# Pooling stage: plain float32 for the group map and for the first half-token up-products, and GpSimd's large operations there on VectorE

## The chip, the cores and the metric

The kernel runs on one core of a Trainium2 chip. The metric is the device time of one execution in microseconds (us); lower is better. The engines have short names in the profile: PE is TensorE's matmul, PEld its weight load, DVE is VectorE, ACT is ScalarE, POOL is GpSimd, SP is the engine that issues the DMAs here.

## What is computed

One step of a two-layer decoder for 512 prompt tokens and 8 sample tokens (520 columns). Layer 0 is a gated linear recurrence (HGRN2), layer 1 a causal pooling mixer; each is followed by a feed-forward with a squared ReLU. All of it is float32. The parts that the change touches:

```python
def _pool(x, hist, start, norm_g, w_grp, scale):
    u = _rmsnorm(x, norm_g)
    ...
    for gi, w in enumerate(POOL_WINDOWS):              # (2, 4, 8, 16), 256 channels each
        ...                                            # trailing-window means of u
        parts.append((hi - lo) / cnt)
    z = (pooled - u)                                   # in 4 groups of 256 channels
    y = jnp.einsum('blgc,gcd->blgd', z, w_grp) * scale
    return y, ext[:, -P:]

def _mlp(x, norm_g, w_up, w_down):
    h = _rmsnorm(x, norm_g)
    a = jnp.square(jax.nn.relu(jnp.einsum('bld,df->blf', h, w_up)))
    return jnp.einsum('blf,fd->bld', a, w_down)

x = x + y;  x = x + _mlp(...)                          # each layer
return _rmsnorm(x, final_norm), ...
```

The group map is linear, so the kernel maps the unpooled channels first, and takes the window means of the mapped rows.

## The kernel before

**Layout.** Channels lie on the 128 partitions, in 8 tiles (`NT`); the 520 columns (`T`) are tokens, in two halves of 260 (`HT`). `x` stays on the chip for the whole run. All weights come as chunks of 128x1024 float32 (512 KB) from one tensor, `wall`, in the order that `_order()` writes out.

**Products.** A product in float32 is made of three fp32r matmuls (`mm3`): both operands are split into a high part (rounded to fp32r) and a low part (the rest), and high·high, high·low and low·high are added up in PSUM. `split()` takes a loaded chunk `w` (pool `raw`, three buffers): ScalarE casts the high part `wh` in two halves, and an engine subtracts for the low part `wl`, VectorE where the second entry of `_order()` is False, GpSimd where it is True. Activations are split in the same way: `split_norm` (gain times `x`, into `u`), `up_part` (into `a`), `unpooled` (into `zh`, `zl`). Split weights and activations share 24 slots of SBUF.

**Order.** `_Mix` is a counter in program time: every few matmuls `tick()` runs what is due of the side work (generators that yield how many ticks to wait), and `top_up()` loads and splits the next chunks. TensorE's order is the order in the program. VectorE's, ScalarE's, GpSimd's and SP's order is written by hand only in the first layer's mixer; from the first feed-forward on a scheduler sets it.

**The stretch in question** starts in the last down-products of the first feed-forward. They are made for one half of the tokens at a time (`pr`, four PSUM buffers), seven or eight for the first half, then eight for the second (three of whose chunks, `AGAIN`, are loaded and split once more). After each, `after_mlp0` adds the squares for the pooling norm (`squares`, sums on GpSimd) and splits the unpooled channels (`unpooled`); after every second one `mapped` does the group map, 12 matmuls for 2x2 tiles. When a half is complete, `rstd` takes the mean by a matmul with `mean_w`, the root on ScalarE and the reciprocal on VectorE (1 / root, `r_p`), and `windows` runs four times: it multiplies by `r_p`, subtracts from `x`, adds shifted copies (1 to 4 adds, `s`), adds the scaled sum to `x`, splits `x` times gain into `u1`, and sums squares for the next norm (`r_m`).

**The second feed-forward** begins with its first group for one half of the tokens at a time: eight up-products of the first half (`up_part`: after the product, VectorE multiplies relu by `r_m` into `t`, ScalarE squares it and casts the high part of `a`, VectorE subtracts the low part), then three down-products (`SOON`) of the first half, then the eight up-products of the second half, with the same up chunks loaded and split a second time. From there on whole products of 520 columns follow.

Lines that the steps of the prediction touch: matmuls L270 and L321 (`mean_w`), `wh` L199, `wl` L194, sums L313, reciprocal L326, `zl` L860, multiplication L889, subtraction L890, window adds L896, scaled sum L899, `u` L297 and L298, `t` L773 and L774, `a` L775 and L776, down-product's add L783.

## Time and profile before

| | us |
|---|---|
| median of 3 runs | 1128.67 |
| lowest and highest | 1127.41, 1131.13 |
| the profiled execution | 1129.82 |
| its span, first to last instruction | 1128.0 |

Over the span PE is busy 1085.1 us (96%), DVE 664.0 (59%), ACT 445.7 (40%), POOL 177.1 (16%). The mean granted clock of TensorE is 0.983 of full speed. Times in the trace count from the first instruction. A busy time is the union of the engine's instructions; a row of a timeline begins with its start and its duration, and ends, in brackets, with how long the engine sat idle before it and what ended that. A DVE instruction's duration reaches some 0.08 us into the next one, so work is best added up from start to start.

### The profile page before, as it was taken

The page shows a single profiled execution, that of the slowest core. Times are in us where ns is not written, and L with a number is a line of the kernel's source. Part 1 is how long each engine was busy: PE and PEld are TensorE (multiplying, and loading weights), DVE is VectorE, ACT ScalarE, POOL GpSimd, SP SyncE. Part 2 cuts the span into 40 slices and gives each one's busy share as a digit, 9 for nine tenths or more (in the row PEclk, how much of TensorE's full clock was granted, in tenths as well). Part 3 has the DMA queues.
Part 4 walks back from the last instruction along what each step waited for, and adds up shares of the span by engine and source line. Part 5 has one row for each costly group of instructions (what it writes and reads, how often), then busy time and mean ns, then how long its engine had stood idle before and what let it go on. Part 6 is the DMA issues. An engine that isn't in the chain of part 4 may idle for free.

```text
span 1128.0 us, 21309 instructions
## 1 busy us (share of the span) xinstructions
PE 1085.1 (96%) x8794; PEld 1071.7 (95%) x8794; DVE 664.0 (59%) x1254; ACT 445.7 (40%) x954; POOL 177.1 (16%) x211
## 2 busy tenths in 40 slices
PE   9899999899999999999999999788999999999996
PEld 8899999899999999999999999687999999999996
DVE  7888888888566433643452466897524524533454
ACT  6544554444344322421431462645514413412442
POOL 1011110011002131322120025584100000000000
PEclk9999999999999999999999999887999999999998
DMA  8233323222244553664461361133512412331212
GB/s 267 77 103 110 98 94 100 80 96 97 80 136 130 184 172 102 182 186 132 156 191 54 103 197 39 57 97 117 183 57 76 144 64 76 110 115 57 94 57 76
DMA packets 67169, 128.13 MB, mean 114 GB/s; under 512 B 8256, under 2 KB 36608, under 8 KB 67072
## 3 DMA queue, kind: packets, MB, share of 16 engines
q1 hardware_dynamic: 67072, 126.77, 35.3%
q8 instruction: 69, 1.13, 0.4%
q14 instruction: 28, 0.23, 0.1%
HBM read 119.71 MB, written 7.50 MB: 113 GB/s over the span
## 4 chain that ended last, share of the span: by engine, by line
PE 73%; DVE 17%; ACT 4%; issue 2%; DMA 1%; POOL 0%; DVEq 0%; POOLq 0%; ACTq 0%
PE acc L270 61%; PE pr L270 10%; DVE A L477 3%; DVE wl L194 2%; DVE s L896 1%; DVE Y L423 1%; DVE z L381 1%; PE pr L472 1%; ACT wh L199 1%; DVE X L423 1%; DMA st<-s 1%; DVE u L298 1%; ACT W L451 1%; DVE W L423 1%; DVE bc L593 1%
## 5 line engine op out<-in xcount | busy, mean ns | idle before, releaser
L270 PE MATMUL acc<-u,wh 128*128 128x260 f32 x2208 | 362.2, 286 | 0.8 <-ACT u L297 0.4
L270 PEld LDWEIGHTS acc<-u,wh 128*128 128x128 f32 x2208 | 304.0, 188 | 2.4 <-DVE u L298 0.8
L270 PE MATMUL acc<-u,wl 128*128 128x260 f32 x1104 | 221.9, 282 | 0.0
L194 DVE TENSOR_TENSOR wl<-w,wh 128x512 fp32r<-128x512 f32 x252 | 179.0, 746 | 40.3 <-ACT wh L199 39.5
L199 ACT CAST wh<-w 128x512 fp32r<-128x512 f32 x276 | 156.2, 617 | 110.3 <-DMA w<-wall 67.4
L270 PEld LDWEIGHTS acc<-u,wl 128*128 128x128 f32 x1104 | 169.8, 188 | 0.0
L270 PE MATMUL acc<-a,wh 128*128 128x260 f32 x1024 | 164.0, 282 | 0.0
L270 PEld LDWEIGHTS acc<-a,wh 128*128 128x128 f32 x1024 | 140.1, 188 | 0.0
L773 DVE SCALAR_TENSOR_TENSOR t<-acc,r 128x520 f32<-128x520 f32 x56 | 39.1, 698 | 120.6 <-PE acc L270 120.5
L774 ACT ACTIVATE t<-t 128x520 f32<-128x520 f32 (+1 forms) x72 | 42.3, 588 | 168.8 <-DVE t L773 168.8
L199 ACT CAST wx<-w 128x512 fp32r<-128x512 f32 x82 | 46.8, 619 | 153.9 <-PE acc L270 150.2
L783 DVE TENSOR_TENSOR x<-x,acc 128x520 f32<-128x520 f32 x48 | 33.3, 694 | 125.2 <-PE acc L270 125.2
L270 PE MATMUL acc<-u,wx 128*128 128x260 f32 x864 | 106.3, 282 | 0.0
L270 PEld LDWEIGHTS acc<-u,wx 128*128 128x128 f32 x864 | 104.6, 188 | 0.0
L270 PE MATMUL acc<-a,wl 128*128 128x260 f32 x512 | 102.9, 282 | 0.0
L270 PE MATMUL acc<-a,wx 128*128 128x260 f32 x768 | 94.6, 282 | 0.0
L270 PEld LDWEIGHTS acc<-a,wx 128*128 128x128 f32 x768 | 93.1, 188 | 0.0
L776 DVE TENSOR_TENSOR a<-t,a 128x520 fp32r<-128x520 f32 (+1 forms) x72 | 48.6, 677 | 58.4 <-ACT a L775 58.4
L270 PEld LDWEIGHTS acc<-a,wl 128*128 128x128 f32 x512 | 78.7, 188 | 0.0
L270 PE MATMUL pr<-a,wh 128*128 128x260 f32 x384 | 71.8, 288 | 0.0
L270 PEld LDWEIGHTS pr<-a,wh 128*128 128x128 f32 x384 | 61.0, 194 | 0.1
L616 POOL TENSOR_TENSOR st<-st,bc 128x512 f32<-128x512 f32 x16 | 21.6, 1348 | 237.8 <-DMA bc<-rows 237.8
(211 smaller groups left out, 1495.1 us busy)
## 6 DMA issues: line engine op xcount, KB each, us to landing
w<-wall SPq DMA_DIRECT2D x181, 512.0 KB, 3.4
st<-s SPq DMA_DIRECT2D x32, 256.0 KB, 3.3
bc<-rows SPq DMA_DIRECT2D x32, 256.0 KB, 6.6
bc<-rows SPq DMA_DIRECT2D x16, 258.0 KB, 3.2
ss_o<-st SPq DMA_DIRECT2D x16, 256.0 KB, 4.2
x<-xT SPq DMA_DIRECT2D x8, 260.0 KB, 5.3
y_o<-pe SPq DMA_DIRECT2D x8, 260.0 KB, 2.6
W<-msk SPq DMA_DIRECT2D x3, 192.0 KB, 6.1
```

The costliest lines, as they stand in the source:

```text
L194: (nc.gpsimd if engine else nc.vector).tensor_tensor(wl[:, k], w[:, k], wh[:, k], op=ALU.subtract)
L199: nc.scalar.copy(wh[:, k], w[:, k])
L270: nc.tensor.matmul(o, lhs[a], r[b], start=first and n == 0, stop=last and n == 2)
L298: nc.vector.scalar_tensor_tensor(u[1][:, s], x[:, i, s], gc, u[0][:, s], op0=ALU.mult, op1=ALU.subtract)
L381: nc.vector.tensor_tensor(wide(z, h), a, wide(r1, h), op=ALU.mult)
L423: nc.vector.tensor_tensor(out, a, R.unsqueeze(len(out.shape) - 1).broadcast_to(out.shape), op=ALU.mult)
L477: nc.vector.copy_predicated(Av[:, jj * kk:(jj + 1) * kk, d:4, :].rearrange("p k s b -> p k (s b)"), mv[:, :, s:s + n, :].rearrange("p k s ...
L616: nc.gpsimd.tensor_tensor(st, st, tf, op=ALU.mult)
L773: nc.vector.scalar_tensor_tensor(wide(t, h), acc, 0.0, wide(r, h), op0=ALU.max, op1=ALU.mult)
L774: nc.scalar.activation(t[:, s], t[:, s], AF.Square)
L776: nc.vector.tensor_tensor(a[m][1][:, s], t[:, s], a[m][0][:, s], op=ALU.subtract)
L783: nc.vector.tensor_tensor(xs, xs, acc, op=ALU.add)
```

## The change

The group map and the eight up-products of the second feed-forward's first group, first token half, become single matmuls in plain float32: the pooling weights are loaded into two tiles of their own and not split, the unpooled channels are one tile `zp` of float32, the first-half `u` is a float32 tile `u32`, and the up chunks of this pass stay whole in their raw buffer until the product is done (`whole_w`). The split of the first half's `u`, which the later groups still need, is made afterwards, as side work (`first_half`). What GpSimd did in this stretch, the low parts of some weights, the sums of squares, the first half's multiplication and all subtractions of `windows`, goes to VectorE; the second entry of `_order()` now says whether a chunk is split.

```diff
-    out = [(i, False) for i in range(down + 2)]
+    out = [(i, True) for i in range(down + 2)]
     out += [(pool + c, None) for c in range(2)]
-    out += [(i, False) for i in range(down + 2, pool)]
+    out += [(i, True) for i in range(down + 2, pool)]
     out += [(i, True) for i in range(down, down + AGAIN)]
-    out += [(mlp1 + m, m > 2) for m in range(G)]
+    out += [(mlp1 + m, False) for m in range(G)]
     out += [(mlp1 + G + m, True) for m in range(SOON)]
-    out += [(mlp1 + m, m % 2 == 0) for m in range(G)]
-    out += [(i, False) for i in range(mlp1 + G + SOON, mlp1 + n)]
+    out += [(mlp1 + m, True) for m in range(G)]
+    out += [(i, True) for i in range(mlp1 + G + SOON, mlp1 + n)]
...
     def load():
         if order:
-            i, engine = order.pop(0)
-            w = rp.tile([P, NT, P], F32, name="w")
+            i, parts = order.pop(0)
+            if parts is None:
+                w = pp.tile([P, NT, P], F32, name="poolw", bufs=2)
+                pool_w.append(w)
+            else:
+                w = rp.tile([P, NT, P], F32, name="w")
+                raw.append((w, parts))
             nc.sync.dma_start(w, wall[i].rearrange("p (k m) -> p k m", m=P))
-            raw.append((w, engine))
...
     def split():
-        w, engine = raw.pop(0)
-        if engine is None:
-            wh, wl = (pp.tile([P, NT, P], F32R, name=n, bufs=2) for n in ("poolwh", "poolwl"))
-        else:
-            wh, wl = slot([P, NT, P], "wh"), slot([P, NT, P], "wl")
+        w, parts = raw.pop(0)
+        if not parts:
+            whole_w.append(w)
+            ahead.append((w,))
+            return
+        wh, wl = slot([P, NT, P], "wh"), slot([P, NT, P], "wl")
...
-                (nc.gpsimd if engine else nc.vector).tensor_tensor(wl[:, k], w[:, k], wh[:, k], op=ALU.subtract)
+                nc.vector.tensor_tensor(wl[:, k], w[:, k], wh[:, k], op=ALU.subtract)
...
-        while order and len(raw) < 2 and len(raw) + halved[0] < 3:
+        while order and len(raw) < 2 and len(raw) + halved[0] + len(whole_w) < 3:
...
         for k in range(NT):
-            mm3(out, [p[:, k, :] for p in w], [[p[:, span(i)] for p in u[k]] for i in hs], k == 0, k == NT - 1)
+            if len(w) == 1:
+                nc.tensor.matmul(out[0], w[0][:, k, :], u[k], start=k == 0, stop=k == NT - 1)
+            else:
+                mm3(out, [p[:, k, :] for p in w], [[p[:, span(i)] for p in u[k]] for i in hs], k == 0, k == NT - 1)
...
-            (add_engine or nc.vector).tensor_tensor(state["sum"][:, s], state["sum"][:, s], sq[:, s], op=ALU.add)
+            nc.vector.tensor_tensor(state["sum"][:, s], state["sum"][:, s], sq[:, s], op=ALU.add)
...
-                acc = use(u, h)
+                acc = use(apart if g == 0 and apart and h == 0 else u, h)
...
-        zh = pp.tile([P, HT + NB], F32R, name="zh", bufs=4)
-        zl = pp.tile([P, HT + NB], F32R, name="zl", bufs=4)
-        gc = vt[:, V_PN + i:V_PN + i + 1]
-        nc.scalar.activation(zh[:, :HT], x[:, i, span(h)], AF.Identity, scale=gc)
-        nc.vector.scalar_tensor_tensor(zl[:, :HT], x[:, i, span(h)], gc, zh[:, :HT], op0=ALU.mult, op1=ALU.subtract)
+        z = zs[i, h] = pp.tile([P, HT + NB], F32, name="zp", bufs=4)
+        nc.scalar.activation(z[:, :HT], x[:, i, span(h)], AF.Identity, scale=vt[:, V_PN + i:V_PN + i + 1])
...
-                mm3([acc[:, m, :n]], [p[:, c, :] for p in w], [[p[:, :n] for p in zs[2 * gi + k, h]]], k == 0, k == 1)
+                nc.tensor.matmul(acc[:, m, :n], pool_w[gi // 2][:, gi % 2 * 4 + m * 2 + k, :], zs[2 * gi + k, h][:, :n], start=k == 0, stop=k == 1)
...
-        (nc.vector if h else nc.gpsimd).tensor_tensor(pg[:, :, HIST:], pg[:, :, HIST:], r_p[:, span(h)].unsqueeze(1).broadcast_to([P, 2, HT]), op=ALU.mult)
-        nc.gpsimd.tensor_tensor(xg, xg, pg[:, :, HIST:], op=ALU.subtract)
+        nc.vector.tensor_tensor(pg[:, :, HIST:], pg[:, :, HIST:], r_p[:, span(h)].unsqueeze(1).broadcast_to([P, 2, HT]), op=ALU.mult)
+        nc.vector.tensor_tensor(xg, xg, pg[:, :, HIST:], op=ALU.subtract)
...
             if h == 0:
-                u1.append(pair("u"))
-            split_norm(u1[i], i, V_M1, h)
-            squares(state_m, np_, i, h, add_engine=nc.gpsimd if h == 0 or n < 2 else nc.vector)
+                nc.scalar.activation(u32[:, i, :], x[:, i, span(0)], AF.Identity, scale=vt[:, V_M1 + i:V_M1 + i + 1])
+            else:
+                u1[i] = pair("u")
+                split_norm(u1[i], i, V_M1, 1)
+            squares(state_m, np_, i, h)
...
+    def first_half():
+
+        for i in range(NT):
+            nc.scalar.copy(u1[i][0][:, span(0)], u32[:, i, :])
+            nc.vector.tensor_tensor(u1[i][1][:, span(0)], u32[:, i, :], u1[i][0][:, span(0)], op=ALU.subtract)
+            yield 2
+        parted.append(True)
...
-        squares(state_p, np_, m, h, add_engine=nc.gpsimd)
+        squares(state_p, np_, m, h)
...
-    mlp(u1, r_m[0], after_mlp1, AGAIN, True)
+    mlp(u1, r_m[0], after_mlp1, AGAIN, [u32[:, i, :] for i in range(NT)])
```

Two more lines go with it: at the end of `pool_half(1)` `first_half` is spawned, and `squares` loses its argument `add_engine`. In the changed kernel the lines have moved: `t` is L785, `a` L788, the sums L325, the reciprocal L338, the multiplication, subtraction and window adds L895, L896 and L902, the scaled sum L905, the few-token sums L909 to L913, the first half's split L949, the matmuls L279 (fp32r), L291 (whole chunk), L880 (group map) and L333 (mean).

How instructions move, first on VectorE. In the program of before, from the reciprocal that scales the first half's up-products (`r_8551`) through the one of the pooling norm's second half (`r_4302`):

```order
L326 RECIPROCAL r_8551<-rs 128x260
L773 SCALAR_TENSOR_TENSOR t<-pr,r_8551 128x260
L776 TENSOR_TENSOR a<-t,a 128x260
L326 RECIPROCAL r_4302<-rs 128x260
L773 SCALAR_TENSOR_TENSOR t<-pr,r_8551 128x260
L889 TENSOR_TENSOR pe<-pe,r_4302 128x2x260 x3
L896 TENSOR_TENSOR s<-pe 128x2x258
L906 TENSOR_TENSOR few<-pe,ph 128x2x8
L889 TENSOR_TENSOR pe<-pe,r_4302 128x2x260
L906 TENSOR_TENSOR few<-pe,ph 128x2x8
L776 TENSOR_TENSOR a<-t,a 128x260
L896 TENSOR_TENSOR s<-s 128x2x256
```

and in the changed program, where the two reciprocals are `r_8464` and `r_4302`:

```order
L338 RECIPROCAL r_8464<-rs 128x260
L785 SCALAR_TENSOR_TENSOR t<-pr,r_8464 128x260
L338 RECIPROCAL r_4302<-rs 128x260
L785 SCALAR_TENSOR_TENSOR t<-pr,r_8464 128x260
L895 TENSOR_TENSOR pe<-pe,r_4302 128x2x260 x3
L896 TENSOR_TENSOR x<-x,pe 128x2x260
L902 TENSOR_TENSOR s<-pe 128x2x258
L912 TENSOR_TENSOR few<-pe,ph 128x2x8
L896 TENSOR_TENSOR x<-x,pe 128x2x260
L912 TENSOR_TENSOR few<-pe,ph 128x2x8
L896 TENSOR_TENSOR x<-x,pe 128x2x260
L895 TENSOR_TENSOR pe<-pe,r_4302 128x2x260
```

The subtractions `x<-x,pe` came in from GpSimd, and no `a` stands between the reciprocals or among these rows any more. The third `t`, three rows further on in the program of before, now stands behind the window work, in this row of VectorE's order:

```order
L788 TENSOR_TENSOR a<-t,a 128x260
L949 TENSOR_TENSOR u<-u_7385,u 128x260 x2
L905 SCALAR_TENSOR_TENSOR x<-s,x 128x2x252
L902 TENSOR_TENSOR s<-pe 128x2x254
L905 SCALAR_TENSOR_TENSOR x<-s,x 128x2x252
L785 SCALAR_TENSOR_TENSOR t<-pr,r_8464 128x260
```

Here the first `a` and two splits of the first half precede it.

On TensorE, around the first up-products, the changed program has, with `u_7385` for `u32` and a whole chunk `w`:

```order
L279 MATMUL pr<-a,wx 128x260 x24
L291 MATMUL pr<-u_7385,w 128x260 x8
L333 MATMUL pr<-sqs,mean_w 128x260
L880 MATMUL acc<-zp,poolw 128x268 x4
L291 MATMUL pr<-u_7385,w 128x260 x4
L333 MATMUL pr<-sqs,mean_w 128x260
L291 MATMUL pr<-u_7385,w 128x260 x4
L880 MATMUL acc<-zp,poolw 128x268 x4
L291 MATMUL pr<-u_7385,w 128x260 x48
L279 MATMUL pr<-a,wx 128x260 x24
```

The places of the group maps, of the two mean matmuls and of the up-products are those of before; each three matmuls of a step have become one.

## Rows read from the trace of the kernel before

**Rows 1.** Shares of the span, from the page: engine, busy us, share, instructions.

```profile
PE 1085.1 (96%) x8794; PEld 1071.7 (95%) x8794; DVE 664.0 (59%) x1254; ACT 445.7 (40%) x954; POOL 177.1 (16%) x211
```

**Rows 2.** Windows: stretch, length, busy us (instructions) by engine, TensorE clock, DMA.

```profile
690.20:729.40 39.20, 30.75 (x213) 29.75 (x212) 35.77 (x60) 18.30 (x53) 23.91 (x21) 0.87 0.15 44
729.40:771.40 42.00, 31.13 (x212) 29.16 (x210) 39.90 (x52) 22.12 (x55) 31.81 (x25) 0.85 0.32 100
771.40:779.60 8.20, 8.18 (x50) 8.18 (x51) 6.53 (x8) 3.64 (x8) 5.34 (x4) 0.71 0.17 64
690.20:779.60 89.40, 70.06 (x472) 67.09 (x471) 82.20 (x119) 44.06 (x114) 61.06 (x49) 0.85 0.23 72
```

**Rows 3.** Waits of TensorE, 660 to 800 us: in all, times, longest.

```profile
PE acc L270 <- DVE zl L860: 5.7, 2, 4.3
PE pr L270 <- DVE a L776: 5.2, 2, 3.6
```

**Rows 4.** Groups of GpSimd, 690.2 to 779.6: busy us, mean ns, idle before.

```profile
L194 POOL TENSOR_TENSOR wl<-w,wh 128x512 fp32r<-128x512 f32 x14 | 19.7, 1430 | 6.4 <-ACT wh L199 6.4
L313 POOL TENSOR_TENSOR sqs<-sqs,sq 128x260 f32<-128x260 f32 x17 | 16.3, 969 | 15.9 <-ACT sq L309 15.6
L890 POOL TENSOR_TENSOR x<-x,pe 128x520 f32<-128x520 f32 x8 | 12.1, 1540 | 0.7 <-DVE few L906 0.7
```

**Rows 5.** Timeline of VectorE: start, duration, instruction, tiles, sizes.

```profile
690.20 1.76 DVE L326 RECIPROCAL r<-rs 128x260 f32<-128x260 f32 x1
739.92 1.70 DVE L896 TENSOR_TENSOR s<-pe 128x516 f32<-128x516 f32 x1
741.54 1.18 DVE L906 TENSOR_TENSOR few<-pe,ph 128x16 f32<-128x16 f32 x1
...
761.70 0.68 DVE L896 TENSOR_TENSOR s<-pe 128x508 f32<-128x508 f32 x1
762.30 0.41 DVE L776 TENSOR_TENSOR a<-t,a 128x260 fp32r<-128x260 f32 x1
762.64 0.67 DVE L899 SCALAR_TENSOR_TENSOR x<-s,x 128x504 f32<-128x504 f32 x1
...
769.41 0.47 DVE L298 SCALAR_TENSOR_TENSOR u<-x,vt,u 128x260 fp32r<-128x260 f32 x1
```

**Rows 6.** Timeline of GpSimd, at 737.78 us.

```profile
737.78 4.92 POOL L890 TENSOR_TENSOR x<-x,pe 128x520 f32<-128x520 f32 x3
```

**Rows 7.** Timeline of TensorE at 782.5 us, loads of L321, loads on the page.

```profile
782.51 0.60 PE L321 MATMUL pr<-sqs,mean_w 128*128 128x260 f32 x2
782.75 0.59 PE L270 MATMUL pr<-u,wh 128*128 128x260 f32 x2
783.18 0.28 PE L270 MATMUL pr<-u,wl 128*128 128x260 f32 x1
783.31 0.40 PE L270 MATMUL pr<-u,wh 128*128 128x260 f32 x2
...
L321 PEld LDWEIGHTS pr<-sqs,mean_w x16: 186/188/334, 337.2 to 1116.9; 128*128 128x128 f32 x16
...
L270 PEld LDWEIGHTS acc<-u,wh 128*128 128x128 f32 x2208 | 304.0, 188 | 2.4 <-DVE u L298 0.8
```

**Rows 8.** Groups of ScalarE, 690.2 to 779.6.

```profile
L309 ACT ACTIVATE sq<-x 128x260 f32<-128x260 f32 x21 | 8.3, 411 | 2.8 <-DVE sqs L313 2.0 <-POOL sqs L313 0.8
L325 ACT ACTIVATE rs<-pr,eps_t 128x260 f32<-128x260 f32 x2 | 1.0, 477 | 3.2 <-PE pr L321 3.2
```

**Rows 9.** DMA issues of the page: queue, KB each, median us to landing.

```profile
w<-wall SPq DMA_DIRECT2D x181, 512.0 KB, 3.4
```

**Rows 10.** TensorE at 219.8 us: a row of the timeline, two windows.

```profile
219.80 2.07 PE L515 MATMUL pr<-vT,kT 128*128 128x128 f32 x8 [2.69 <-ACT kT L510]
...
219.80:223.20 3.40, 3.40 (x17) 3.06 (x18) 2.44 (x7) 2.42 (x5) 0.58 (x2) 0.50 0.53 154
223.20:225.00 1.80, 1.80 (x16) 1.80 (x16) 1.33 (x5) 1.29 (x5) 0.00 (x0) 1.00 0.03 7
```

More of the change, by code (lines that the diff above doesn't have):

```diff
@@ L156, in free @@
     def free(w):
+        if len(w) == 1:
+            whole_w.remove(w[0])
+            return
         for t in w:
@@ L171, in _kernel @@
     raw, ahead, halved = [], [], [0]
+    whole_w = []
     depth = [DEPTH]
@@ L199, in split @@
             nc.scalar.copy(wh[:, k], w[:, k])
-        mix.spawn(low(1 if mix.now > 16 and not engine and mix.now < 230 else 0))
-        (pool_w if engine is None else ahead).append((wh, wl))
+        mix.spawn(low(1 if 16 < mix.now < 230 else 0))
+        ahead.append((wh, wl))
     def top_up():
-        while raw and len(ahead) < depth[0] and taken[0] + 2 <= SLOTS + len(extra):
+        while raw and len(ahead) < depth[0] and (taken[0] + 2 <= SLOTS + len(extra) or not raw[0][1]):
             split()
-        while order and len(raw) < 2 and len(raw) + halved[0] < 3:
+        while order and len(raw) < 2 and len(raw) + halved[0] + len(whole_w) < 3:
             load()
@@ L280, in product @@
         for k in range(NT):
-            mm3(out, [p[:, k, :] for p in w], [[p[:, span(i)] for p in u[k]] for i in hs], k == 0, k == NT - 1)
+            if len(w) == 1:
+                nc.tensor.matmul(out[0], w[0][:, k, :], u[k], start=k == 0, stop=k == NT - 1)
+            else:
+                mm3(out, [p[:, k, :] for p in w], [[p[:, span(i)] for p in u[k]] for i in hs], k == 0, k == NT - 1)
             if (k + 1) % step == 0:
@@ L298, in split_norm, with squares @@
         nc.vector.scalar_tensor_tensor(u[1][:, s], x[:, i, s], gc, u[0][:, s], op0=ALU.mult, op1=ALU.subtract)
-    def squares(state, pool, i, h=None, add_engine=None, apart=False):
+    def squares(state, pool, i, h=None, apart=False):
         s = span(h)
@@ L341, in _kernel @@
     uin, parts = [], []
-    if True:
-        for i in range(NT):
-            uin.append(pair("u"))
-            split_norm(uin[i], i, V_HN)
-        split()
-        for i, (n, b) in enumerate((("og", 1), ("z", 3), ("z", 3), ("sg", 2), ("sg", 2), ("f", 1), ("k", 1), ("gs", 1))):
-            t = hp.tile([P, T], F32, name=n, bufs=b)
-            parts.append(t)
-            if i % 4 == 3:
-                nc.vector.tensor_tensor(t, x[:, i, :], x[:, i, :], op=ALU.mult)
-            else:
-                nc.scalar.activation(t, x[:, i, :], AF.Square)
-            if i % 2:
-                nc.vector.tensor_tensor(t, t, parts[i - 1], op=ALU.add)
+    for i in range(NT):
+        uin.append(pair("u"))
+        split_norm(uin[i], i, V_HN)
+    split()
+    for i, (n, b) in enumerate((("og", 1), ("z", 3), ("z", 3), ("sg", 2), ("sg", 2), ("f", 1), ("k", 1), ("gs", 1))):
+        t = hp.tile([P, T], F32, name=n, bufs=b)
+        parts.append(t)
+        if i % 4 == 3:
+            nc.vector.tensor_tensor(t, x[:, i, :], x[:, i, :], op=ALU.mult)
+        else:
+            nc.scalar.activation(t, x[:, i, :], AF.Square)
+        if i % 2:
+            nc.vector.tensor_tensor(t, t, parts[i - 1], op=ALU.add)
     load()
@@ L756, in _kernel, with mlp @@
     steady.enter_context(tc.manual_schedule(engines={mybir.EngineType.SP}))
-    def mlp(u, r, after, full, apart=False, before_last=None):
+    def mlp(u, r, after, full, apart=None, before_last=None):
         for g in range(NF // G):
@@ L762, in mlp @@
                 before_last()
+            assert not (apart and g == 1) or parted
             a = []
             def up_part(m, h):
-                acc = use(u, h)
+                acc = use(apart if g == 0 and apart and h == 0 else u, h)
                 def rest():
@@ L834, in _kernel @@
     hsum = cp.tile([P, NT, NB], F32, name="hsum")
-    pp = pe = ph = None
+    pp = pe = ph = u32 = None
     def open_pool():
-        nonlocal pp, pe, ph
+        nonlocal pp, pe, ph, u32
         assert not states
@@ L846, in open_pool @@
         ph = pp.tile([P, NT, NB], F32, name="ph")
+        u32 = pp.tile([P, NT, HT], F32, name="u32")
     for gi, w in enumerate(WINS):
@@ L909, in windows @@
             if h == 0:
[L910 to L912 removed]
+                nc.scalar.activation(u32[:, i, :], x[:, i, span(0)], AF.Identity, scale=vt[:, V_M1 + i:V_M1 + i + 1])
+            else:
+                u1[i] = pair("u")
+                split_norm(u1[i], i, V_M1, 1)
+            squares(state_m, np_, i, h)
     def pool_states():
@@ L932, in pool_half @@
             r_m.append(new_r())
+        else:
+            mix.spawn(first_half(), 4)
         mix.spawn(rstd(r_m[0], state_m, np_, (h,)), 8 if h == 0 else 14)
+    def first_half():
+        for i in range(NT):
+            nc.scalar.copy(u1[i][0][:, span(0)], u32[:, i, :])
+            nc.vector.tensor_tensor(u1[i][1][:, span(0)], u32[:, i, :], u1[i][0][:, span(0)], op=ALU.subtract)
+            yield 2
+        parted.append(True)
+    parted = []
     done = [set(), set()]
     def after_mlp0(m, h):
-        squares(state_p, np_, m, h, add_engine=nc.gpsimd)
+        squares(state_p, np_, m, h)
         unpooled(m, h)
```

9 lines of the change are left out of this document (3 added, 6 removed).

## The prediction

> **What bounds the kernel now.** I read the page's shares first: TensorE is busy 96% of the 1128.0 us span, VectorE 59% [rows 1]. That average hides one stretch. I then cut the trace at the places that the change touches, and three stages show there [rows 2]: from the first pooling reciprocal at 690.2 us to the reciprocal that scales the first up-products (729.4), from there to the last `a` of the first half-token group (771.4), and the three down-products behind it, up to 779.6, where the second half's up-products begin. In these 89.4 us the reader is to see VectorE busy 82.2 us and TensorE only 70.1, at a mean granted clock of 0.87, 0.85 and 0.71 of full speed. So here VectorE sets the pace, TensorE waits for it, and TensorE's clock falls for a part of the time. The waits name the same thing: TensorE's two longest are for VectorE's `zl` and VectorE's `a` [rows 3]. Outside the stretch nothing that the diff touches is on the path.
>
> Why VectorE is so slow there is in the single instructions. The 508-wide add at 761.70 takes 0.68 us, and the next instruction starts 0.60 later; the 516-wide add at 739.92, the same line, takes 1.70, and the next starts 1.62 later [rows 5]. What differs is GpSimd: at 739.92 it is in the middle of three 1.6 us subtractions (737.78 to 742.70) [rows 6]. The instructions that VectorE runs beside GpSimd are about 1 us longer each. GpSimd issues 17 sums, 8 subtractions and 18 weight halves (14 are in the group shown, 4 under another tile name) besides smaller things in the stretch [rows 4].
>
> **TensorE's work after the change.** A plain float32 matmul shows up as two records. Between the first at 782.51 and the `wl` matmul at 783.18 lie two of them and two fp32r matmuls; an fp32r matmul costs 0.12 (0.36 for the three of a product step), so the plain one costs 0.67 - 0.24 = 0.43 us, against 0.36 for the three that it replaces [rows 7]. That is a loss: 64 up-product matmuls take 27.8 us instead of 23.0, and a group map of four takes 1.74 instead of 1.44 (1.8 at 268 columns).
>
> Here a rule speaks against the change. Weight loads of 128x128 take 188 ns in plain float32 (median) as in fp32r (mean) [rows 7], and stay hidden under a pass of 0.22 us. The Trainium skill, "TensorE: Matmul & The Clock Gate", section "Weight-path perf modes — Fast Weight Load (FWL) and DoubleRow", has the fast weight load on only where the input is not FP32, which would make plain float32 loads slower than others. The rows here don't show it, so the sum goes by 188 ns; by the rule it would be the second rival below.
>
> From 690.2 on TensorE then has: the rest of the last first-half map, delayed by 0.9 us (three earlier maps, 0.3 each), to 692.6; six down-products of 24 matmuls (17.2) and two maps (3.6), to 713.4; eight up-products (27.8), two maps (3.6) and two row-mean matmuls (0.9); three down-products (8.6). Without any wait the second half would begin at 754.3. The before trace has it at 779.6, so 25.3 us is the most that the change can gain.
>
> **VectorE's work after the change**, by start-to-start times of instructions that GpSimd does not touch: 0.60 for 504 to 520 elements, 0.34 for 260, 0.40 for the scaled 260-wide one (0.47 with the same 0.08 overlap), 1.7 for a reciprocal [rows 5], some 0.09 for tiny ones; weight halves count like 512 elements. ScalarE's square is 0.41, its square root 0.48 [rows 8].
>
> First stage. The change takes out the zl instructions and the u splits of the first half, and adds four multiplications, four subtractions and the sums. In its program order VectorE has, from reciprocal to reciprocal: one reciprocal, 7 down-product adds, 4 + 4 + 10 + 4 wide ones, 8 tiny, 14 sums, one split: 1.7 + 2.4 + 13.2 + 0.7 + 4.8 + 0.3 = 23.1 us, instead of 39.2. It now fits under TensorE, whose last down-product ends at 713.4. Behind that stand one add, then squares and sums in turn over two buffers (about 4 us), the row-mean matmul and the root (0.9): the second reciprocal starts at 719.0. The stage takes 28.8 instead of 39.2, and TensorE runs through it.
>
> Second stage. r ready at 720.7; TensorE does a map and half an up-product, the row-mean of the other half at 721.7, root and reciprocal to 724.4, and is through the second up-product. VectorE then goes through the second half's windows before it comes back to the third `t`: from the second `t` to the third, 4 + 4 multiplications and subtractions, 9 adds, 3 scaled ones, 2 u splits, 8 tiny, and five 260-wide with the `t` itself: 15.2 us, so it comes at 739.9. The `pr` pool has four buffers: up-products three to six are done at 738.8, the seventh must wait for that `t` (1.2 us). The next `t` follow after 4.2 and 4.7 us of VectorE work (splits of the first half, u, sums, halves of weights), so the eighth and the first down-product wait about 1 us each; the last `a` is there at 754.2. The stage takes 35.2 instead of 42.0. ScalarE's casts for the down weights sit in this chain; their weights wait for a raw buffer until the sixth up-product is done (738.8) and land 3.4 us after their issue [rows 9], before ScalarE comes to them at about 744.
>
> Third stage. Three down-products at full clock end 6.0 us later instead of 8.2. The halves of the second half's weights that leave GpSimd cost VectorE 8 x 0.6 = 4.8 us more under 23 us of up-products: hidden; if that cover were gone, 4.8 us. Before 690.2 VectorE takes over 7 sums and 6 halves (2.4 + 3.6 us) and loses 8 zl (3.2); TensorE does not wait there now, and I count it at nothing; uncovered it would be 2.8 us.
>
> Sum: 10.4 + 6.8 + 2.2 = 19.4 us. I take off 2 us, because each handover between engines costs something that these sums leave out, and because one short fall of the clock would cost about that. 17.4 us off the profiled execution's own 1129.82 us give 1112.4; this execution lies 1.15 above the median of the runs, so 1111 us.
>
> **The rivals.** *Slower, first way: VectorE is not long because of GpSimd.* Then the moved instructions join the queue that sets the end at their present length. In the stretch some 12 wide ones at 1.1, 17 sums at about 1.1, 8 splits at 0.6 and 12 halves at 0.75 come to 46, what is taken out (8 zl, 8 u, 6 halves, small ones) to 20: 26 us more, some 7 of them hidden: 1148 us. It decides as soon as the moved ones are no shorter than now. Against it: the same line takes 0.68 and 1.70 [rows 5], and the short ones are those with GpSimd idle. 3 in 100.
>
> *Slower, second way: plain float32 costs TensorE more than the few matmuls of before tell.* There are 84 such matmuls in the stretch, nearly back to back. At 17.4 / 84 = 0.21 more each, 0.64 instead of 0.43, the gain is gone. At half clock they cost 0.87: 36 us more, 6 of them in place of waits, 1142 us. If a load took twice 188 ns and two loads per matmul set the pace, 0.75 each: 27 us more, some 1132 to 1138. This is what the cited rule on fast weight loads would bring. For it: no stretch of before has such products. Against it: the clock. After a wait of 2.69 us it stood at 0.50 from 219.8 to 223.2, TensorE began it with 2.07 us of plain float32 matmuls, and at 223.2 it was back at full speed [rows 10]. 4 in 100.
>
> *No change within 0.3%* (about what a measurement of this kernel can tell; 1125.3 to 1132.1): the waits move but stay, for instance since the third `t` now stands behind the whole window work, later in VectorE's order than before. It needs another 14 us in VectorE's 64 rows between the reciprocal and the last `a`, 0.2 us each. 5 in 100.
>
> *A smaller gain*: handovers of 0.08 us on some 110 instructions take 9 us back, or the clock stays low through the second stage, where half speed for 10 us of work costs 5 to 10: 1118 to 1125. 18 in 100.
>
> **How the numbers follow.** The forecast (1104 to 1118) has 70 in 100, the smaller gain 18, no change 5, slower 7. Faster by over 0.3%: 0.88, the same 0.05, slower 0.07. The range goes from 1104, close to the ceiling (1128.7 - 25.3 = 1103.4), to 1122, which takes in the forecast and over half of the smaller gain, 8 in 10.
>
> **What would show it.** Right: the 504 to 520-wide lines at 0.68 throughout, no 260-wide one but the reciprocal above 0.5; the second half's first up-product near 761 us; the group maps at 1.74 and the up-products at 3.47; waits of 1 us for `t` at the seventh and eighth up-product and the first down-product; a granted clock near 1.0 over the whole stretch. Wrong: wide VectorE instructions of over 1 us without GpSimd, up-products well over 3.5 us, or a clock of 0.5 in them; a long wait of ScalarE for the down weights would put my smaller gain in the place of the forecast. GpSimd should be nearly idle from 690 us on.

## The result, and the profile after

| | us |
|---|---|
| before, median of 4 runs (lowest, highest) | 1128.29 (1127.41, 1131.13) |
| changed, median of 4 runs (lowest, highest) | 1111.24 (1111.10, 1111.35) |
| ratio, with its 95% interval | 0.9845 (0.9827 to 0.9862) |
| span of the profiled execution, before and changed | 1128.0, 1109.0 |

The change makes the kernel 17 us faster, with 1111 forecast. Run once more beside the experiments, the same changed kernel took 1110.82 us against 1129.59 for the kernel before: 0.9836 (0.9823 to 0.9849), 18.8 us. The two ratios agree within their intervals; the median of before differs between the two sets.

The first view is the page's line of shares, which answers to [rows 1]: engine, busy us, share, instructions.

```profile
PE 1081.6 (98%) x8698; PEld 1063.4 (96%) x8698; DVE 643.9 (58%) x1276; ACT 438.0 (39%) x942; POOL 95.5 (9%) x145
```

TensorE is busy 98% instead of 96%, and GpSimd has lost half of its work. VectorE took that work over and lost the splits, and is busy 20 us less in all.

The second view cuts the changed trace at the same places as [rows 2]: the first pooling reciprocal, the reciprocal that scales the first up-products, the end of the last `a`, the first up-product of the second half. Columns: stretch, length, then busy us (instructions) of PE, PEld, DVE, ACT and POOL, the granted clock, DMA share and GB/s.

```profile
690.48:718.49 28.01, 28.01 (x198) 26.56 (x197) 24.19 (x54) 16.16 (x48) 0.00 (x0) 1.00 0.06 20
718.49:754.67 36.18, 32.29 (x150) 26.54 (x148) 34.22 (x74) 19.23 (x54) 1.41 (x2) 1.00 0.48 134
754.67:760.86 6.19, 6.19 (x53) 6.14 (x52) 4.46 (x8) 2.76 (x6) 0.00 (x0) 1.00 0.74 232
690.48:760.86 70.38, 66.49 (x397) 59.24 (x396) 62.87 (x135) 38.15 (x106) 1.41 (x2) 1.00 0.34 97
```

The stretch is 70.4 us long instead of 89.4, so the 19.0 us between the spans all come from here. The first stage went from 39.2 to 28.0, the second from 42.0 to 36.2, the third from 8.2 to 6.2. In the first, TensorE now works without a gap and VectorE fits under it. The clock is 1.00 throughout.

The third view lists TensorE's waits from 660 to 800 us, as [rows 3] did: in all, times, longest.

```profile
PE pr L291 <- DVE t L785: 1.4, 2, 1.0
PE pr L279 <- DVE t L785: 1.0, 1, 1.0
PE pr L279 <- ACT a L787: 0.7, 1, 0.7
PE pr L291 <- DMA w<-wall: 0.3, 1, 0.3
PE pr L279 <- DVE a L788: 0.3, 1, 0.3
```

3.7 us of waits are left, and the largest are for `t`, as forecast. The last view of the changed kernel is VectorE's timeline (start, duration, instruction, tiles, sizes), to be held against [rows 5]:

```profile
727.53 0.68 DVE L902 TENSOR_TENSOR s<-pe 128x516 f32<-128x516 f32 x1
728.14 0.16 DVE L912 TENSOR_TENSOR few<-pe,ph 128x16 f32<-128x16 f32 x1
...
740.04 0.41 DVE L785 SCALAR_TENSOR_TENSOR t<-pr,r 128x260 f32<-128x260 f32 x1
```

The 516-wide add behind the pooling norm's second half took 1.70 us before and takes 0.68 now; the tiny instruction of 128x16 fell from 1.18 to 0.16.

### The profile page after: what moved, and what is told of

Same layout as the page of the kernel before. It is cut to its first block, busy times and chain, and to the rows that moved or that the text cites. A ratio compares the mean times of both kernels' runs of the same rounds, so it can differ in the third digit from the quotient of the medians.

```text
span 1109.0 us, 21023 instructions
## 1 busy us (share of the span) xinstructions
PE 1081.6 (98%) x8698; PEld 1063.4 (96%) x8698; DVE 643.9 (58%) x1276; ACT 438.0 (39%) x942; POOL 95.5 (9%) x145
## 3 DMA queue, kind: packets, MB, share of 16 engines
q1 hardware_dynamic: 67072, 126.77, 35.8%
## 4 chain that ended last, share of the span: by engine, by line
PE 77%; DVE 13%; ACT 4%; DMA 1%; issue 1%; DVEq 0%; POOL 0%; ACTq 0%
PE acc L279 61%; PE pr L279 11%; DVE A L488 3%; DVE wl L203 2%; PE pr L291 1%; PE acc L880 1%; DVE Y L434 1%; DMA w<-wall 1%; DVE z L392 1%; PE pr L483 1%; ACT wh L208 1%; DVE X L434 1%; ACT W L462 1%; DVE W L434 1%; DVE bc L604 1%
## 5 line engine op out<-in xcount | busy, mean ns | idle before, releaser
L279 PE MATMUL acc<-u,wh 128*128 128x260 f32 x2208 | 362.7, 286 | 0.6 <-DVE u L310 0.6
L279 PEld LDWEIGHTS acc<-u,wh 128*128 128x128 f32 x2208 | 304.6, 189 | 1.9 <-DVE u L310 1.0
L279 PE MATMUL acc<-u,wl 128*128 128x260 f32 x1104 | 222.1, 282 | 0.0
L203 DVE TENSOR_TENSOR wl<-w,wh 128x512 fp32r<-128x512 f32 x264 | 185.5, 739 | 47.0 <-ACT wh L208 46.0
L208 ACT CAST wh<-w 128x512 fp32r<-128x512 f32 x264 | 149.3, 618 | 111.3 <-DMA w<-wall 66.9
L279 PEld LDWEIGHTS acc<-u,wl 128*128 128x128 f32 x1104 | 169.9, 188 | 0.0
L279 PE MATMUL acc<-a,wh 128*128 128x260 f32 x1024 | 164.2, 282 | 0.0
L279 PEld LDWEIGHTS acc<-a,wh 128*128 128x128 f32 x1024 | 140.2, 188 | 0.0
L785 DVE SCALAR_TENSOR_TENSOR t<-acc,r 128x520 f32<-128x520 f32 x56 | 39.1, 699 | 124.9 <-PE acc L279 124.7
L279 PE MATMUL acc<-u,wx 128*128 128x260 f32 x864 | 106.2, 282 | 0.0
L795 DVE TENSOR_TENSOR x<-x,acc 128x520 f32<-128x520 f32 x48 | 33.3, 693 | 124.6 <-PE acc L279 124.6
L279 PEld LDWEIGHTS acc<-u,wx 128*128 128x128 f32 x864 | 104.5, 188 | 0.0
L279 PE MATMUL acc<-a,wl 128*128 128x260 f32 x512 | 102.8, 282 | 0.0
L279 PE MATMUL acc<-a,wx 128*128 128x260 f32 x768 | 94.6, 282 | 0.0
L279 PEld LDWEIGHTS acc<-a,wx 128*128 128x128 f32 x768 | 93.1, 188 | 0.0
L788 DVE TENSOR_TENSOR a<-t,a 128x520 fp32r<-128x520 f32 (+1 forms) x72 | 46.7, 649 | 55.6 <-ACT a L787 55.4
L279 PEld LDWEIGHTS acc<-a,wl 128*128 128x128 f32 x512 | 78.8, 188 | 0.0
L279 PE MATMUL pr<-a,wh 128*128 128x260 f32 x384 | 70.8, 286 | 0.0
L279 PEld LDWEIGHTS pr<-a,wh 128*128 128x128 f32 x384 | 59.6, 188 | 0.4
L279 PE MATMUL pr<-a,wl 128*128 128x260 f32 x192 | 54.2, 282 | 0.0
```

The source lines that it names most:

```text
L203: nc.vector.tensor_tensor(wl[:, k], w[:, k], wh[:, k], op=ALU.subtract)
L208: nc.scalar.copy(wh[:, k], w[:, k])
L279: nc.tensor.matmul(o, lhs[a], r[b], start=first and n == 0, stop=last and n == 2)
L785: nc.vector.scalar_tensor_tensor(wide(t, h), acc, 0.0, wide(r, h), op0=ALU.max, op1=ALU.mult)
L788: nc.vector.tensor_tensor(a[m][1][:, s], t[:, s], a[m][0][:, s], op=ALU.subtract)
L795: nc.vector.tensor_tensor(xs, xs, acc, op=ALU.add)
```

## Theories

Mine: VectorE sets the end of this stretch, and it is slow there because GpSimd works beside it. The gain comes from GpSimd going quiet; plain float32 takes splits away that VectorE would not have had time for, and costs TensorE 0.6 us a product. The rival: the gain comes from the splits that are spared, and where sums and subtractions run matters little. A second rival: VectorE's long instructions had another cause than GpSimd, and they shrank with it by coincidence.

All kernels are compared over one stretch, from the first pooling reciprocal to the reciprocal that scales the second half's up-products. Behind it they take 339.5 to 340.5 us to the last instruction (the first hand order alone 348.9), so one line for each holds nearly the whole difference. The columns are those of the windows above: stretch, length, busy PE, PEld, DVE, ACT, POOL, clock, DMA, GB/s. The kernel before:

```profile
690.20:784.18 93.98, 74.64 (x509) 71.61 (x508) 82.62 (x120) 45.58 (x117) 61.92 (x50) 0.85 0.25 80
```

and the changed kernel:

```profile
690.48:765.67 75.19, 71.30 (x435) 63.99 (x434) 64.50 (x138) 39.67 (x109) 1.41 (x2) 1.00 0.34 100
```

Each experiment shows its own such line. It was timed beside runs of the kernel before on the same chip, and its gain is taken against those (medians of 1129.59 to 1129.83 us). One of the runs was the changed kernel itself, as a base:

> The changed kernel once more, beside the others on one chip, as their base: 1111 us.

It took 1110.82 us.

## Experiment 1: float32 alone

The changed kernel, but GpSimd keeps what it did.

```diff
-    out += [(mlp1 + m, True) for m in range(G)]
+    out += [(mlp1 + m, 2 if m % 2 == 0 else True) for m in range(G)]
...
-                nc.vector.tensor_tensor(wl[:, k], w[:, k], wh[:, k], op=ALU.subtract)
+                (nc.gpsimd if parts == 2 else nc.vector).tensor_tensor(wl[:, k], w[:, k], wh[:, k], op=ALU.subtract)
...
-        nc.vector.tensor_tensor(xg, xg, pg[:, :, HIST:], op=ALU.subtract)
+        nc.gpsimd.tensor_tensor(xg, xg, pg[:, :, HIST:], op=ALU.subtract)
```

where 2 stands for a chunk whose low part is GpSimd's (those of `AGAIN` and `SOON` too); and so for the first half's multiplication and for the sums.

> The float32 half of the change alone: map and first up-products in plain float32, while GpSimd keeps its weight halves, sums, multiplications and subtractions. Contention theory (most of the gain comes from GpSimd leaving VectorE alone): VectorE's wide instructions stay at 1.1 to 1.7 us beside GpSimd, so the run gains at most 7 of the 17 us, 1121 or more. Sparing theory (most of the gain comes from the splits that VectorE no longer makes): 10 us or more, 1118 or less.

Measured: 1118.57 us, 0.9901 (0.9885 to 0.9918), a gain of 11.1. The window:

```profile
691.86:775.66 83.80, 74.34 (x433) 66.53 (x432) 62.50 (x100) 39.58 (x109) 51.54 (x41) 0.96 0.29 90
```

By its gain that is on the sparing theory's side (10 or more), by its time just short of it (1118). The figure that I gave for my own theory, a gain of at most 7, is missed: float32 alone brings over half of what the change brings. GpSimd's work is not quite what it was, though. Ten weight halves of the first up chunks, which GpSimd made before, are made by no engine here, and it is busy 51.5 us in the stretch instead of 61.9. (The profiled execution took 1121.04 us, the longest of the four.) The part up to the second reciprocal, the one that scales the first up-products:

```profile
691.86:722.82 30.96, 29.34 (x202) 27.40 (x201) 22.61 (x32) 15.94 (x48) 23.62 (x22) 1.00 0.11 35
```

It takes 31.0 us instead of 39.2 [rows 2], a gain of 8.2, though GpSimd is busy there as long as before. Behind it, up to the end of the stretch, the gain is 2.0 (52.8 us instead of 54.8).

GpSimd still holds VectorE up. VectorE's timeline in the first stage:

```profile
698.17 0.41 DVE L795 TENSOR_TENSOR x<-x,pr 128x260 f32<-128x260 f32 x1
698.51 1.38 DVE L902 TENSOR_TENSOR s<-s 128x520 f32<-128x520 f32 x1
699.92 1.15 DVE L909 TENSOR_TENSOR few<-s,kt 128x8 f32<-128x8 f32 x1
```

GpSimd's at the same time:

```profile
697.57 1.75 POOL L896 TENSOR_TENSOR x<-x,pe 128x520 f32<-128x520 f32 x1
699.28 1.77 POOL L895 TENSOR_TENSOR pe<-pe,r 128x520 f32<-128x520 f32 x1
```

The down-product's add (L795, one input from PSUM) takes 0.41 us under GpSimd's subtraction; the window add that follows, with both inputs in SBUF, takes 1.38, and an instruction of 128x8 takes 1.15.

## Experiment 2: the move alone

The kernel before, with every weight half, sum, multiplication and subtraction of GpSimd's on VectorE; all products stay split.

```diff
-    out += [(mlp1 + m, m > 2) for m in range(G)]
+    out += [(mlp1 + m, False) for m in range(G)]
...
-        nc.gpsimd.tensor_tensor(xg, xg, pg[:, :, HIST:], op=ALU.subtract)
+        nc.vector.tensor_tensor(xg, xg, pg[:, :, HIST:], op=ALU.subtract)
...
-        squares(state_p, np_, m, h, add_engine=nc.gpsimd)
+        squares(state_p, np_, m, h)
```

and so for the other entries and the first half's multiplication.

> The other half alone: GpSimd's sums, weight halves, multiplications and subtractions go to VectorE, every product keeps its three matmuls, and all splits stay. Contention theory: wide instructions at 0.68 us, VectorE's first stage 39 to about 30 us, the second held up by 16 weight halves of 0.6 us; 8 to 13 us gained, 1116 to 1121. Sparing theory: VectorE has more to do and is the bound, so no gain or a loss, 1126 to 1148.

Measured: 1116.01 us, 0.9881 (0.9867 to 0.9896), a gain of 13.6. The window:

```profile
689.55:771.48 81.93, 69.52 (x519) 68.05 (x518) 76.77 (x167) 46.51 (x117) 1.47 (x2) 0.90 0.30 92
```

The sparing theory, which wanted no gain or a loss, falls: VectorE has some 14 us more work in the stretch than in experiment 1 (76.8 busy, 62.5 there), and the stretch is 2 us shorter. It is still too much for the first stage, as TensorE's waits from 690 to 800 us show:

```profile
PE pr L270 <- ACT wh L199: 7.6, 1, 7.6
PE pr L270 <- DVE a L776: 4.8, 2, 3.3
```

The wait of 7.6 us is for the high part of the first up chunk. ScalarE casts it at 719.09, after the `u` of the last windows, and that one waited for VectorE's `x` until 717.65. So what is named ScalarE is VectorE's row of work.

The part up to the second reciprocal:

```profile
689.55:726.70 37.15, 29.55 (x220) 29.05 (x219) 34.64 (x82) 20.02 (x55) 0.00 (x0) 0.86 0.21 62
```

It takes 37.2 us, where the expectation had about 30: a gain of only 2.0, with GpSimd idle. Behind it the gain is 10.0 (44.8 us instead of 54.8).

The two halves of the change gain 11.1 and 13.6 us alone, 24.7 in all, and 18.8 together. The windows, which are of single executions, make 22.2 us of the 24.7, and by them the two do not overlap in the first stage: up to the second reciprocal they gain 8.2 and 2.0 alone, and 11.2 together. They overlap behind it, with 2.0 and 10.0 alone and 7.6 together (54.8 to 47.2 us). Experiment 3 shows why: once GpSimd is quiet, the float32 up-products cost more there than they save.

## Experiment 3: map in float32 and the move, up-products split

```diff
-    mlp(u1, r_m[0], after_mlp1, AGAIN, [u32[:, i, :] for i in range(NT)])
+    mlp(u1, r_m[0], after_mlp1, AGAIN, u1)
```

and the chunks and the first half's `u` are split as before the change.

> The change without float32 up-products: group map in float32, GpSimd's work on VectorE, but up chunks and first-half u are split as before. TensorE saves 8 x 0.6 = 4.8 us, VectorE gets 16 weight halves of 0.6 us (9.6) in the second stage, and the splits of u in the first (3.2). If VectorE sets the end there, 2 to 7 us slower than the changed kernel, 1113 to 1118; if TensorE does, up to 5 us faster, 1106.

Measured: 1114.01 us, 0.9862 (0.9847 to 0.9876), a gain of 15.6. The window:

```profile
690.63:768.50 77.87, 69.53 (x499) 66.71 (x498) 74.03 (x154) 46.10 (x117) 1.47 (x2) 0.93 0.32 97
```

The stretch is 2.7 us longer than in the changed kernel. So the float32 map is worth 4.1 us on top of the move (81.9 to 77.9), and the float32 up-products another 2.7, though they cost TensorE 4.8 us of matmuls. The part up to the second reciprocal:

```profile
690.63:723.75 33.12, 29.45 (x206) 28.05 (x205) 31.48 (x69) 19.70 (x55) 0.00 (x0) 0.95 0.20 64
```

The second reciprocal comes 33.1 us after the first instead of 28.0. VectorE is busy 31.5 us here, against 24.2 in the changed kernel, and TensorE waits 3.5 us for the high half of the first up chunk. Behind this reciprocal it is the other way round: 44.8 us here, 47.2 in the changed kernel. So the time lies where the expectation had it for VectorE as the bound, but not for its reason, 16 weight halves that hold up the second stage. The float32 up-products gain 5.1 us in the first stage, before they run, because their chunks and the first half's `u` are not split there, and lose 2.4 in the part where they run. Whether fewer of them in float32 would do better, no run tried.

## Experiment 4: GpSimd reading beside VectorE, and nothing else

The changed kernel, and in each of the eight calls of `windows` two multiplications on GpSimd in a scratch tile that nothing reads.

```diff
+        for _ in range(2):
+            nc.gpsimd.tensor_tensor(scr, scr, r_p[:, span(h)].unsqueeze(1).broadcast_to([P, 2, HT]), op=ALU.mult)
```

> The changed kernel with 16 multiplications of 128x520 put on GpSimd, two per call of windows, into a scratch tile that nobody reads: VectorE's work is the same, only the company is new. Contention theory: VectorE's wide instructions beside them take 1.1 to 1.7 us instead of 0.68, about 1 us for each GpSimd instruction; the 8 of the second stage have no slack to hide in, so 1117 to 1127. Rival (before's long instructions had another cause, such as what VectorE itself waited for): 0.68 throughout and 1111.

Measured: 1127.56 us, 0.9984 (0.9975 to 0.9993). Sixteen instructions that nobody waits for take 16.7 us of the 18.8 back, just above the upper end of what was expected. The window, and its part up to the second reciprocal:

```profile
691.12:783.20 92.08, 75.08 (x435) 66.88 (x434) 82.00 (x139) 39.55 (x109) 27.53 (x18) 0.93 0.28 82
691.12:727.26 36.14, 30.55 (x198) 28.29 (x197) 32.94 (x53) 16.04 (x48) 12.74 (x8) 0.91 0.05 16
```

The stretch is 92.1 us instead of 75.2; TensorE has the same 435 matmuls. The expectation spoke of no slack in the second stage only; the eight instructions of the first cost as much, 36.1 us instead of 28.0. VectorE's timeline at the second pooling reciprocal:

```profile
736.79 1.77 DVE L898 TENSOR_TENSOR x<-x,pe 128x520 f32<-128x520 f32 x1
738.49 1.77 DVE L906 TENSOR_TENSOR s<-pe 128x516 f32<-128x516 f32 x1
740.19 1.25 DVE L916 TENSOR_TENSOR few<-pe,ph 128x16 f32<-128x16 f32 x1
741.37 0.69 DVE L898 TENSOR_TENSOR x<-x,pe 128x520 f32<-128x520 f32 x1
```

and GpSimd's there:

```profile
736.28 12.10 POOL L900 TENSOR_TENSOR scr<-scr,r 128x520 f32<-128x520 f32 x7
```

VectorE's long instructions start 1.70 apart, GpSimd's seven take 1.73 each: the two engines take turns. The price is per instruction, not per element: 1.08 us more for the 520-wide one (0.69 to 1.77) and 1.09 for the 128x16 one (0.16 to 1.25). One VectorE instruction pays for each of GpSimd's: the 520-wide one at 741.37, right behind the 128x16 one that paid, takes its 0.69. The second rival, another cause for the long instructions, falls.

## Experiment 5: GpSimd writing beside VectorE

As experiment 4, with memsets in place of the multiplications (and one tiny reader for each call, so that they run at the same time).

```diff
+        nc.gpsimd.tensor_tensor(scr[:, :, :2], scr[:, :, :2], r_p[:, span(h)][:, :2].unsqueeze(1).broadcast_to([P, 2, 2]), op=ALU.mult)
+        for _ in range(4):
+            nc.gpsimd.memset(scr, 0.0)
```

> As the run with the reading multiplications, but GpSimd only fills the scratch tile (four 128x520 memsets per call of windows) and reads next to nothing. If it is GpSimd's reading of SBUF that holds VectorE up: VectorE's instructions stay at 0.68 us and the time is 1111. If any GpSimd work on SBUF does it: as long as with the multiplications, 1117 or more.

Measured: 1110.58 us, 0.9834 (0.9821 to 0.9846), the changed kernel's time. The window:

```profile
689.90:765.10 75.20, 71.29 (x435) 63.98 (x434) 64.53 (x138) 39.68 (x109) 27.88 (x42) 1.00 0.33 100
```

GpSimd is busy 27.9 us in the stretch, as much as in experiment 4 (27.5), and VectorE's busy time stays at 64.5. So it is not GpSimd's being busy that costs, but its reading of SBUF. GpSimd's timeline shows the other side:

```profile
734.77 4.86 POOL L899 TENSOR_TENSOR scr<-scr,r 128x4 f32<-128x4 f32 x1
```

The tiny reader of 128x4 takes 4.86 us, for as long as VectorE runs a row of instructions with two inputs in SBUF; it ends in the `t` (one input from PSUM) that VectorE starts at 739.49.

## Experiments 6 to 8: the waits that are left

Three kernels try to take the last 3.7 us of waits away. The first puts the split of the first half's `u` off until the second half's up-products:

```diff
-            mix.spawn(first_half(), 4)
+            mix.spawn(first_half(), 26)
...
-            nc.scalar.copy(u1[i][0][:, span(0)], u32[:, i, :])
+            nc.scalar.activation(u1[i][0][:, span(0)], u32[:, i, :], AF.Identity, bias=zero)
```

where `zero` is 0 times the second half's `r_m`, so that the cast cannot come earlier.

> The changed kernel with the first half's split (eight 260-wide subtractions of 0.34 us, eight casts on ScalarE) put off until the second half's up-products. If VectorE's row of work between the two reciprocals and the last a sets the waits of about 1 us for t there, 1 to 2 us faster than the changed kernel, 1109 to 1110; if the splits fill gaps, the same, 1111.

Measured: 1110.83 us, 0.9834 (0.9819 to 0.9848): by the median the changed kernel's time, 1110.82. But no execution took just that: two took 1109.46 and 1109.78 us, as expected if VectorE's row sets the waits, and two 1111.89 and 1112.00, with a slightly lower mean granted clock (0.994 instead of 0.996). The profile is of the last one. The window:

```profile
691.46:765.92 74.46, 72.49 (x435) 65.67 (x434) 61.60 (x130) 36.76 (x101) 1.41 (x2) 0.98 0.35 101
```

The waits did fall, to 2.1 us, and the last `a` ended 61.9 us after the first pooling reciprocal instead of 64.2. But in two windows of the trace, around the end of the last wait, the clock went:

```profile
750.00:754.20 4.20, 2.90 (x18) 2.08 (x17) 3.84 (x9) 4.17 (x11) 0.00 (x0) 1.00 0.37 132
754.20:757.60 3.40, 3.40 (x19) 3.40 (x18) 2.77 (x6) 1.83 (x4) 0.00 (x0) 0.51 0.83 253
```

After 1.3 us of idle time in the first window TensorE worked 3.4 us at half speed (1.2 instead of 2.4 GHz), which is some 1.7 us of work. The changed kernel waits a little longer there and keeps its clock. Why it does, these runs don't tell, and there is no profile of the two shorter executions.

The other two write VectorE's order by hand from the first up-product on: each `t` straight behind one call of `windows`, its `a` one product later, the second half's `u` and sums behind them.

```diff
+                hand.enter_context(tc.manual_schedule(engines={mybir.EngineType.DVE}))
...
-                    nc.vector.tensor_tensor(a[m][1][:, s], t[:, s], a[m][0][:, s], op=ALU.subtract)
+                    if lows:
+                        lows.pop()()
+                    lows.append(low)
```

> The changed kernel with VectorE's order written by hand from the first up-product on: each t straight behind one window set, its a one product later, and the second half's u splits, its sums and the first half's split put behind them. Working through VectorE's rows, the third t comes near 736 instead of 740 us, and the last a near 750 instead of 754.7. If the 3.9 us that TensorE still waits are due to VectorE's order: 3 to 4 us faster than the changed kernel, 1107 to 1108. If VectorE's amount of work sets the end whatever its order, or waits of VectorE on ScalarE take the place: 1111 or more.

Measured: 1124.65 us, 0.9956 (0.9943 to 0.9968), under the last of the expectations and far above its 1111. The window:

```profile
690.41:770.64 80.23, 73.85 (x433) 66.63 (x432) 61.85 (x129) 37.68 (x101) 2.10 (x2) 0.96 0.32 94
```

The third `t` came at 738.53 and the wait for `t` is gone, but TensorE's longest wait up to the second half's reciprocal is for what I had put behind:

```profile
PE pr L279 <- DVE wx L203: 4.7, 1, 4.7
```

Another 9 us went behind the landmark, where TensorE waited some 4 us for weight halves and casts and ran two stretches of 3.4 us at half speed. The second hand order moves the down chunks' halves ahead of the last `t`, the `u` and sums behind the last `a`, and ends with the first half's down-products.

> The hand order again, with what held TensorE up in the first one put right: the down chunks' low halves stand ahead of the last t, the second half's u splits and sums behind the last a, and the hand order ends with the first half's down-products. If VectorE's order was behind the 3.9 us of TensorE's waits in the changed kernel, waits below 2 us up to the second half's first up-product and 1107 to 1109; if the late u splits only shift the wait to that product, 1110 to 1113; if a row in order costs more than the scheduler's mixed one, slower than that.

Measured: 1115.04 us, 0.9874 (0.9857 to 0.9890), longer than the first two expectations allow. The window:

```profile
691.80:768.96 77.16, 71.61 (x435) 64.31 (x434) 63.25 (x130) 37.71 (x101) 2.10 (x2) 1.00 0.32 97
```

TensorE's longest wait in it:

```profile
PE pr L279 <- DVE wl L203: 3.7, 2, 3.3
```

Again no wait for `t`, and again the loss turned up at the weights.

Two rows show what the fixed order pays for: VectorE stood behind an `a` whose cast ScalarE could not make, as ScalarE itself stood behind a cast of weights that had not landed. VectorE's:

```profile
747.81 0.43 DVE L790 TENSOR_TENSOR a<-t,a 128x260 fp32r<-128x260 f32 x1 [2.24 <-ACT a L787]
```

and ScalarE's, two microseconds earlier:

```profile
745.88 1.14 ACT L208 CAST wx<-w 128x512 fp32r<-128x512 f32 x2 [4.64 <-DMA w<-wall]
```

So a fixed order moved the waits for `t` to other places, and by its median no version beat the changed kernel.

## Why the prediction held, point by point

**The bound.** Right: VectorE set the pace. All 19.0 us of span came out of the stretch that [rows 2] marked, and adding GpSimd's company alone (experiment 4) put 16.7 us back. The prediction named TensorE's two longest waits of before. The same view has three more, 3.9 us in all, in which TensorE waits for GpSimd's own results:

```profile
PE pr L270 <- POOL wl L194: 1.6, 2, 1.1
PE pr L321 <- POOL sqs L313: 1.5, 1, 1.5
PE pr L270 <- POOL wx L194: 0.8, 1, 0.8
```

The move takes these away as well, and no run parts them from the shorter VectorE instructions in its 13.6 us.

**Float32 on TensorE.** Right to 1%. The chain of the changed trace has an up-product, loads and all, at 3.51 us (forecast 3.47), and a group map at 1.75 and, 268 wide, 1.81 (forecast 1.74, 1.8):

```profile
714.00 3.51 PE pr L291 x16
...
719.75 1.75 PE pr L291 x8
...
723.69 1.81 PE acc L880 x8
```

(an x16 is one up-product of eight matmuls, two records each; the x8 at 719.75 is half of one.) The loads of plain float32 are as fast as those of fp32r [rows 7], over 128 of them (shortest, median, longest in ns):

```profile
L291 PEld LDWEIGHTS pr<-u,w x128: 186/190/190, 713.7 to 748.5; 128*128 128x128 f32 x128
```

So the Trainium skill's rule on fast weight loads ("TensorE: Matmul & The Clock Gate", "Weight-path perf modes — Fast Weight Load (FWL) and DoubleRow"), which the second rival cited, shows no cost here: 190 ns against 188. Whether the fp32r loads are fast ones in the page's sense, no row tells.

**First stage.** Forecast 28.8 us, measured 28.0; the second reciprocal at 718.49 (719.0 said). **Second stage.** Forecast 35.2, measured 36.2; the third `t` at 740.04 (739.9), the last `a` done at 754.67 (754.2), and waits for `t` where they were named: 1.0 us each at the eighth up-product and the first down-product, 0.4 instead of 1.2 at the seventh. **Third stage.** Forecast 6.0, measured 6.2. In sum 70.4 against 70.0: the second half's first up-product at 760.86, where 761 was named.

**What was off.** The allowance of 2 us for handovers and a fall of the clock: the stretch needed 0.4 of it. So the term was 1.6 us too large. That the forecast of 1111 still came out at 1111.24 is due to the base: the sum took 1.15 us off, since the profiled execution lay that much above the median of three runs, but in the later sets the median of before was 1129.6 to 1129.8, within 0.2 of that execution's 1129.82. The two errors nearly cancel.

The down weights were to be issued at 738.8, to land 3.4 us later [rows 9] and to hide. They were issued at 740.14, landed 3.39 us later, and ScalarE stood idle 0.4 us for them. The load before them in the chain, a whole up chunk, takes over twice as long, which the prediction had not thought of:

```profile
729.03 7.20 DMA w<-wall
...
736.37 3.76 PE pr L291 x16
...
740.14 3.39 DMA w<-wall
```

and ScalarE's row:

```profile
743.55 1.14 ACT L208 CAST wx<-w 128x512 fp32r<-128x512 f32 x2 [0.40 <-DMA w<-wall]
```

The long load was issued behind the writes of the pooling state; that these held it up is not shown. It cost the sixth up-product 0.3 us; in the second hand order a load of this stage held ScalarE up for 4.64.

**The reason behind it** was told too widely. The prediction said that VectorE's instructions beside GpSimd are about 1 us longer each. Only those with two inputs in SBUF are. Already in the trace of before, in the stretch with GpSimd busiest, the eight `t` (one input from PSUM) show no trace of it, while of the eight `a` (both in SBUF) two take 1.15 and 1.48 us (shortest, median, longest in ns):

```profile
L773 DVE SCALAR_TENSOR_TENSOR t<-pr,r x8: 366/416/429, 731.2 to 769.1; 128x260 f32<-128x260 f32 x8
L776 DVE TENSOR_TENSOR a<-t,a x8: 415/416/1483, 732.6 to 770.9; 128x260 fp32r<-128x260 f32 x8
```

It made no difference to the sum, since what the change moves and keeps on VectorE in the stretch is nearly all of the second kind.

It was also told for the whole stretch. In experiment 2 GpSimd is idle in the first stage, and VectorE is still busy 34.6 us of its 37.2, against 35.8 of 39.2 before [rows 2]. So there GpSimd's company cost VectorE little more than the work that it takes over does, and most of the gain came with the work that float32 spares. The prediction's sum for this stage counts that work; its reason leaves it out. In the second stage the reason holds as told.

**The rivals.** Slower because VectorE's length had nothing to do with GpSimd: excluded by experiments 4 and 5. Slower because float32 costs TensorE more: excluded by the 3.51 us. No change: VectorE's rows between reciprocal and last `a` came within 1 us of the sum. The smaller gain: the stretch came out 0.4 us over the sum, handovers and all, and the clock stayed at 1.00.

## What to carry to other kernels

Before work is spread over VectorE and GpSimd, look at how long the same instruction of VectorE takes with GpSimd idle and with GpSimd reading SBUF; here a GpSimd instruction of 1.7 us lengthened one VectorE instruction by 1.1, however small that was, and cost more than the 0.6 that it took over. A saving on one engine is worth what the next bound leaves of it: two halves of 11.1 and 13.6 us made 18.8, since the float32 up-products gained 5.1 us ahead of the place where they run and lost 2.4 there. Where in a stretch a part of the change gains is read from landmarks inside it. Waits that are left on an engine which is full can be moved by another order, but three tries gained nothing by their medians.

## What the runs showed of the hardware

VectorE and GpSimd take turns where VectorE's instruction has two inputs in SBUF and GpSimd's reads SBUF, and in no other pair that these runs hold: 16 readers cost 16.7 us, memsets of the same busy time nothing, and the `t` and `x` adds with an input from PSUM keep their 0.41 us. This is what the Trainium skill states in "SBUF — State Buffer", section "Who interferes with whom", and each part of it that these runs touch agrees. By the page, what the two engines share is an exclusive lock, which fits the price by instruction. Long readers took turns with VectorE one by one (experiment 4), while a reader of 128x4 waited out a whole row of VectorE instructions, 4.86 us (experiment 5); what decides between the two, the runs leave open.

ScalarE can hold VectorE up in another way. In the second hand order it stood idle 4.64 us at a cast of weights that had not landed; the square and the cast for a `t` that VectorE had started at 745.13 came only behind that cast, at 746.92 and 747.37, and VectorE's `a` at 747.81.
